# A hybrid decoder trunk: attention's 256-column products as three fp32r products, with the residual kept in DRAM meanwhile

## The chip, the cores and the metric

The kernel runs on one core of a Trainium2 chip. The metric is the device time of one execution in microseconds (us), as the median of several runs. Engines are called by the profile's names: PE is TensorE (matrix products; PEld its loads of the stationary operand), DVE is VectorE, ACT is ScalarE, POOL is GpSimd, SP is SyncE, whose queue issues nearly all DMAs here. SBUF is the on-chip memory of 128 partitions, PSUM the memory that products are written to.

## The reference

Two layers on 256 tokens of width 2048, in float32. Layer 0 mixes tokens with a gated MLP, layer 1 with a "forgetting" attention; a convolutional FFN of width 5632 follows each, and a last norm ends it. The change touches the attention of layer 1 only: 16 heads of 128 columns, two blocks of 128 queries, causal.

```
for i in range(S // Q_BLOCK):          # two query blocks
    lo, hi = i * Q_BLOCK, (i + 1) * Q_BLOCK
    s = einsum(q[lo:hi], k[:hi]) * scale + c[lo:hi, None] - c[None, :hi]
    p = softmax(where(causal, s, -inf))
    outs.append(einsum(p, v[:hi]))
o = concat(outs) * sigmoid(g);  h = h + o @ w_out
```

So a head has three 128 x 128 blocks of scores: queries 0-127 against keys 0-127, and queries 128-255 against both halves of the keys.

## The kernel before

**The stream.** All large weights pass through one stream of chunks of 128 x 1024 floats (512 KB). `Stream.run` goes through them: it issues the load of the chunk six ahead (SP), splits the chunk three ahead into a rounded part `whi` (ACT, L112) and a remainder `wlo` (DVE, L113), both of the type fp32r, then issues the products of the current chunk (PE, L213), and then calls `advance`, which takes every unfinished side task (a Python generator) one step, in the order in which they were started. The instructions of a step stand on each engine's queue behind the split that was issued just before it. A weight product in full accuracy is three fp32r products (rounded by rounded, rounded by remainder, remainder by rounded); after 24 such products of 256 columns a chunk is done. There are four buffers for parts, so the split of the chunk three ahead begins once the PE is through with the chunk before the current one.

**The attention's side task.** `heads` is started just before the chunks of the value projection (kvf_v: 32 chunks in four blocks of 512 columns) and goes on into the gate projection (b_g). It works in rounds, one every four chunks: rounds 0 to 7 issue the score products of two heads and start a `softmax` task for each; from some round on a round also issues the value products of up to two heads whose weights have come back transposed. In a round the order on PE is: value products (L1164 to L1166: three products of 128 columns a head), then for each head the score products (L1170: first query block against 128 keys, L1171: second against 256). All are plain fp32 products. The output goes from PSUM to `q`'s place by ACT (L1174).

**Softmax.** The even head's task reads the scores from PSUM one advance after the round (DVE L1122, then row maxima L1124), takes exponentials one advance later (ACT L1127), and normalises (L1129, L1131), transposes in blocks of 32 (L949) and sends the rows through DRAM (SP, L956 and L960) after that. The odd head's task does the same two advances later, so its score reading falls into the last advance before the next round. The two score buffers in PSUM (`mp`) are reused every round: a round's odd scores need the reading of the odd scores of the round before. Evictions of the value projection's blocks (ACT L1052) fall right behind the rounds 1, 3, 5 and 7, since a block has eight chunks. The key normalisation of the last key block (L1016 to L1025, L949) runs while the first chunks of kvf_v are streamed.

**The residual.** `h` ([128, 16, 256] float32, 2 MB) stays in SBUF from the input to the output. It is read by `kv_operand` before the attention and next read and written by `residual` in the output projection (b_out) after the gate projection.

Of the kernel before, what the change touches and what calls it, by code (L numbers as in the profile page):

```python
# [10 lines left out]
F32 = mybir.dt.float32  # L11
F32R = mybir.dt.float32r
# [5 lines left out]
P = 128  # L18
# [116 lines left out]
class Phase:  # L135


    def __init__(self, tc):
        self.tc, self.ctx, self.pool, self.name = tc, None, None, None

    def open(self, name):
        if self.name == name:
            return
        self.close()
        self.ctx = ExitStack()
        self.pool = self.ctx.enter_context(self.tc.tile_pool(name=name, bufs=1))
        self.name, self.kept = name, {}
# [30 lines left out]
def build(ctx, tc, d, out):  # L178
# [10 lines left out]
    h = const.tile([P, KD, T], F32, name="h")  # L189
# [201 lines left out]
    def residual(p, gain, scale=token_scale):  # L391

        def done(ps, both):
            hh = h[:, 2 * p:2 * p + 2, :]
# [577 lines left out]
    def kv_operand():  # L972
        assert state["prepared"]
        att("X2")
        nc.vector.tensor_tensor(att("gain"), column(C_QNORM), column(C_KNORM), op=OP.mult)
        for _ in range(3):
            yield
        for kt in range(KD):
            prep(att("X2"), kt, C_KVNORM)
            for _ in range(1 + kt % 2):  # L980
                yield

# [123 lines left out]
    def heads():  # L1106

        q, k, v, ccol = att("q"), att("k"), att("v"), att("ccol")
        rows, waiting = {}, []
# [26 lines left out]

        for hd in range(2):
            fetch(hd)
        for _ in range(3):
            yield  # L1140
        n = 0
        while state["done"] < NH:
# [11 lines left out]
            go = [hd for hd, _ in waiting if hd < state["v"]][:2]  # L1154
            if not pair and len(go) < min(2, NH - state["done"]):
                yield
                continue
            if go or pair:
                between()
            o = main_ps()[:, 0, :] if go else None  # L1160
            for i, hd in enumerate(go):
                pT = waiting.pop(0)[1]
                oo, vv = o[:, i * T:(i + 1) * T], v[:, :, hd * P:(hd + 1) * P]
                nc.tensor.matmul(oo[:, :P], vv[:, 0, :], pT[:, :, 0, :], start=True, stop=True)  # L1164
                nc.tensor.matmul(oo[:, P:], vv[:, 0, :], pT[:, :, 1, :], start=True, stop=False)  # L1165
                nc.tensor.matmul(oo[:, P:], vv[:, 1, :], pT[:, :, 2, :], start=False, stop=True)  # L1166
            for hd, L in pair.items():
                S = misc_ps()[:, :3 * P]
                kk = k[:, hd // 4, :, hd % 4, :]
                nc.tensor.matmul(S[:, :P], q[:, hd, :P], kk[:, :4], start=True, stop=True)  # L1170
                nc.tensor.matmul(S[:, P:], q[:, hd, P:], kk, start=True, stop=True)  # L1171
                s.start(softmax(hd, S, L))
            for i, hd in enumerate(go):
                nc.scalar.activation(q[:, hd, :], o[:, i * T:(i + 1) * T], AF.Copy)  # L1174
                state["done"] += 1
            for _ in range(4):
                yield
            n += 2

# [16 lines left out]
    state = {"normed": False, "layer": 0, "v": 0, "done": 0, "gates": 0, "mixed": 0, "scaled": 0, "summed": 0, "added": 0,  # L1196
             "prepared": False, "wide": [8, 2]}
    cd = dram.tile([NH, T], F32, name="cd")

# [52 lines left out]
    ph.close()  # L1252

# [67 lines left out]
```

## Time and profile before

| | |
|---|---|
| median of 3 runs | 2165.07 us (2164.87 to 2165.72) |
| profiled execution | 2165.71 us |
| its span on the core | 2164.0 us |
| instructions | 45230 |
| mean granted TensorE clock | 0.999 |
| read and written in HBM | 432.29 and 15.22 MB |
| score products L1170, L1171 | first at 1173.55 us, last round at 1267 us |
| value products L1164 | 1198.1 to 1303.9 us |

A page of the profile names groups by source line, engine, operation and tiles (out<-in). Products overlap at their ends, so the pitch from start to start is what one costs. An idle time and its releaser stand in brackets behind the row that followed it. A product in fp32 shows as two records, one in fp32r as one.

### The profile page before, as it was taken

The page shows a single profiled execution, that of the slowest core. Times are in us where ns is not written, and L with a number is a line of the kernel's source. Part 1 is how long each engine was busy: PE and PEld are TensorE (multiplying, and loading weights), DVE is VectorE, ACT ScalarE, POOL GpSimd, SP SyncE. Part 2 cuts the span into 40 slices and gives each one's busy share as a digit, 9 for nine tenths or more (in the row PEclk, how much of TensorE's full clock was granted, in tenths as well). Part 3 has the DMA queues.
Part 4 walks back from the last instruction along what each step waited for, and adds up shares of the span by engine and source line. Part 5 has one row for each costly group of instructions (what it writes and reads, how often), then busy time and mean ns, then how long its engine had stood idle before and what let it go on. Part 6 is the DMA issues. An engine that isn't in the chain of part 4 may idle for free.

```text
span 2164.0 us, 45230 instructions
## 1 busy us (share of the span) xinstructions
PE 2154.6 (100%) x18572; PEld 2137.7 (99%) x18572; DVE 1632.0 (75%) x2362; ACT 1199.0 (55%) x1644; POOL 27.5 (1%) x46
## 2 busy tenths in 40 slices
PE   9999999999999999999999999999999999999998
PEld 9999999999999999999999999999999999999998
DVE  6696687777777699977777676668777777779997
ACT  6664455555555555554545665545555555555555
POOL 0000000000000000000001200000000000000000
PEclk9999999999999999999999999999999999999999
DMA  8686566666666567677778876666766666666665
GB/s 313 188 248 199 194 198 194 192 196 188 202 195 192 175 199 227 224 230 185 243 233 268 238 218 200 189 217 200 266 195 194 192 195 192 196 192 186 205 205 166
DMA packets 157551, 450.47 MB, mean 208 GB/s; under 512 B 26064, under 2 KB 48352, under 8 KB 156960
## 3 DMA queue, kind: packets, MB, share of 16 engines
q1 hardware_dynamic: 155808, 443.63, 65.8%
q0 software_dynamic: 1072, 3.41, 0.6%
q8 instruction: 145, 2.38, 0.5%
q10 hardware_dynamic: 464, 0.55, 0.1%
q14 instruction: 62, 0.51, 0.1%
HBM read 432.29 MB, written 15.22 MB: 207 GB/s over the span
## 4 chain that ended last, share of the span: by engine, by line
PE 99%; DVE 0%; ACT 0%; issue 0%; POOL 0%; DVEq 0%; ACTq 0%; POOLq 0%
PE ps L213 97%; PE mp L213 1%; PE mp L1171 0%; PE mp L776 0%; PE ps L1165 0%; PE ps L1166 0%; PE ps L1164 0%; PE mp L1170 0%; ACT sq L437 0%; DVE h L743 0%; DVE h L436 0%; DVE h L737 0%; PE mp L408 0%; ACT fin_t L729 0%; DVE fin_t L733 0%
## 5 line engine op out<-in xcount | busy, mean ns | idle before, releaser
L113 DVE TENSOR_TENSOR wlo<-raw,whi 128x1024 fp32r<-128x1024 f32 (+1 forms) x732 | 887.8, 1219 | 287.1 <-ACT whi L112 283.9
L112 ACT ACTIVATE whi<-raw 128x1024 fp32r<-128x1024 f32 (+1 forms) x732 | 770.2, 1058 | 589.5 <-PE ps L213 471.4
L213 PE MATMUL ps<-X,whi 128*128 128x256 f32 (+1 forms) x6466 | 823.7, 280 | 0.0
L213 PEld LDWEIGHTS ps<-X,whi 128*128 128x128 f32 x6466 | 775.4, 188 | 6.8
L213 PE MATMUL ps<-X,wlo 128*128 128x256 f32 x3328 | 445.1, 276 | 0.0
L213 PEld LDWEIGHTS ps<-X,wlo 128*128 128x128 f32 x3328 | 409.8, 188 | 1.7
L213 PE MATMUL ps<-whi,ffn_H 128*128 128x256 f32 (+1 forms) x1852 | 303.2, 277 | 0.0
L213 PEld LDWEIGHTS ps<-whi,ffn_H 128*128 128x128 f32 x1852 | 255.5, 188 | 0.7
L213 PE MATMUL ps<-whi,X 128*128 128x256 f32 (+1 forms) x1336 | 221.5, 279 | 0.0
L213 PE MATMUL ps<-wlo,ffn_H 128*128 128x256 f32 (+1 forms) x924 | 192.1, 277 | 0.0
L213 PEld LDWEIGHTS ps<-whi,X 128*128 128x128 f32 x1336 | 187.3, 188 | 1.4
L920 DVE SCALAR_TENSOR_TENSOR ffn_room<-ffn_room,col 128x255 f32<-128x255 f32 x352 | 161.9, 481 | 6.4
L213 PE MATMUL ps<-whi,att_X 128*128 128x256 f32 (+2 forms) x970 | 164.3, 285 | 0.0
L213 PEld LDWEIGHTS ps<-wlo,ffn_H 128*128 128x128 f32 x924 | 144.2, 188 | 0.2
L213 PE MATMUL ps<-wlo,X 128*128 128x256 f32 (+1 forms) x666 | 144.3, 279 | 0.0
L389 DVE TENSOR_TENSOR ffn_room<-ps,rB 128x512 f32<-128x512 f32 x76 | 52.5, 691 | 114.4 <-PE ps L213 114.4
L213 PEld LDWEIGHTS ps<-whi,att_X 128*128 128x128 f32 x970 | 135.3, 188 | 3.5
L916 ACT ACTIVATE ffn_room<-ffn_room,col 128x256 f32<-128x256 f32 x176 | 96.3, 595 | 53.2 <-DVE ffn_room L389 53.2
L213 PEld LDWEIGHTS ps<-wlo,X 128*128 128x128 f32 x666 | 106.3, 188 | 0.4
L213 PE MATMUL ps<-wlo,att_X 128*128 128x256 f32 (+2 forms) x476 | 105.4, 286 | 0.0
L90 ACT ACTIVATE whi<-raw 128x768 fp32r<-128x768 f32 x46 | 39.0, 848 | 68.0 <-PE ps L213 54.7
L213 PEld LDWEIGHTS ps<-wlo,att_X 128*128 128x128 f32 x476 | 75.4, 188 | 1.0
(223 smaller groups left out, 1669.1 us busy)
## 6 DMA issues: line engine op xcount, KB each, us to landing
raw<-up SPq DMA_DIRECT2D x352, 512.0 KB, 4.2
raw<-down SPq DMA_DIRECT2D x154, 512.0 KB, 4.2
raw<-a_in_u SPq DMA_DIRECT2D x32, 512.0 KB, 4.4
raw<-a_out SPq DMA_DIRECT2D x32, 512.0 KB, 3.9
raw<-b_q SPq DMA_DIRECT2D x32, 512.0 KB, 4.7
raw<-kvf_v SPq DMA_DIRECT2D x32, 512.0 KB, 4.9
raw<-b_g SPq DMA_DIRECT2D x32, 512.0 KB, 4.2
raw<-b_out SPq DMA_DIRECT2D x32, 512.0 KB, 3.9
```

Source lines behind the costliest of these rows:

```text
L90: self.nc.scalar.activation(hi[:, cols], src[:, cols], AF.Copy)
L112: self.nc.scalar.activation(h, raw, AF.Copy)
L113: self.nc.vector.tensor_tensor(l, raw, h.bitcast(F32), op=OP.subtract)
L213: nc.tensor.matmul(o, a, b, start=start, stop=stop, skip_group_check=True)
L389: nc.vector.tensor_tensor(a, src, rB[:, None, :].to_broadcast([P, 2, T]), op=OP.mult)
L916: nc.scalar.activation(c[:, m, :], a[:, m, :], AF.Identity, scale=w[2], bias=column(C_CONVB + l * 2 * KF + f))
L920: nc.vector.scalar_tensor_tensor(c[:, m, n:], a[:, m, :T - n], w[k], c[:, m, n:], op0=OP.mult, op1=OP.add)
```

## The change

1. In a round, the products of 256 columns are made as three fp32r products. On the score side that is the second query block against all 256 keys. On the value side the first value block meets both query blocks' weights, so that two products of 128 columns become one of 256 (three in fp32r). The second value block (128 columns) and the first query block's scores (128 columns) stay in fp32.
2. The rounded parts are written by ACT, the remainders by DVE: for queries and keys in `query_parts`, for values and weights in `weight_parts`. Both are called in the four steps between two rounds, where there were four bare `yield`s. One set of buffers each, shared by the two heads of a round.
3. On PE all fp32r products of a round come first, value side before score side, and then the fp32 ones.
4. The heads of a round's value products are fixed earlier, when their parts are made, so the first value products come in round 3 and not in round 2.
5. The parts need room in SBUF. `h` moves into a pool of its own on the other side of SBUF, is stored in DRAM in eight DMAs by `kv_operand` (after its last reading, two advances apart), gives its place to the parts, and is loaded back in eight DMAs when `heads` is through.

```diff
+    side = Phase(tc, "right")
+    side.open("h0")
+    h = side.keep("h", [P, KD, T])
...
+        for i in range(8):
+            yield
+            yield
+            nc.sync.dma_start(kept[:, 2 * i:2 * i + 2, :], h[:, 2 * i:2 * i + 2, :])
+        state["kept"] = True
+
+    def taken_back():
+        nonlocal h
+        side.open("h1")
+        h = side.keep("h", [P, KD, T])
+        for i in range(8):
+            yield
+            nc.sync.dma_start(h[:, 2 * i:2 * i + 2, :], kept[:, 2 * i:2 * i + 2, :])
+        state["kept"] = False
...
+        def query_parts(n):
+
+            qq, kk = q[:, n:n + 2, P:], k[:, n // 4, :, n % 4:n % 4 + 2, :].rearrange("p t h j -> p h t j")
+            kv = [kp[:, i].rearrange("p h (t j) -> p h t j", t=8) for i in range(2)]
+            nc.scalar.activation(qp[:, 0], qq, AF.Copy)
+            nc.scalar.activation(kv[0], kk, AF.Copy)
+            yield
+            nc.vector.tensor_tensor(qp[:, 1], qq, qp[:, 0].bitcast(F32), op=OP.subtract)
+            nc.vector.tensor_tensor(kv[1], kk, kv[0].bitcast(F32), op=OP.subtract)
+
+        def weight_parts():
+
+            take = [hd for hd, _ in waiting if hd < state["v"]][:2]
...
+                nc.scalar.activation(vp[:, 0, i], v[:, 0, hd * P:(hd + 1) * P], AF.Copy)
+                nc.scalar.activation(pp[:, 0, i].rearrange("p (b r j) -> p r b j", b=2, r=4), pT[:, :, :2, :], AF.Copy)
+            yield
...
+                nc.vector.tensor_tensor(vp[:, 1, i], v[:, 0, hd * P:(hd + 1) * P], vp[:, 0, i].bitcast(F32),
+                                        op=OP.subtract)
+                hi, lo = (pp[:, l, i].rearrange("p (b r j) -> p r b j", b=2, r=4) for l in range(2))
+                nc.vector.tensor_tensor(lo, pT[:, :, :2, :], hi.bitcast(F32), op=OP.subtract)
+
+        def three(o, stat, mov, start, stop):
+            for j, (x, y) in enumerate(((0, 0), (0, 1), (1, 0))):
+                mm(o, stat[:, x], mov[:, y], start and j == 0, stop and j == 2)
...
-        for _ in range(3):
-            yield
+        yield
+        yield from query_parts(0)
+        yield
...
-            for i, hd in enumerate(go):
-                pT = waiting.pop(0)[1]
-                oo, vv = o[:, i * T:(i + 1) * T], v[:, :, hd * P:(hd + 1) * P]
-                nc.tensor.matmul(oo[:, :P], vv[:, 0, :], pT[:, :, 0, :], start=True, stop=True)
-                nc.tensor.matmul(oo[:, P:], vv[:, 0, :], pT[:, :, 1, :], start=True, stop=False)
-                nc.tensor.matmul(oo[:, P:], vv[:, 1, :], pT[:, :, 2, :], start=False, stop=True)
+            S = {hd: misc_ps()[:, :3 * P] for hd in pair}
+            for i, (hd, pT) in enumerate(go):
+                three(o[:, i * T:(i + 1) * T], vp[:, :, hd % 2], pp[:, :, hd % 2], i == 0, False)
+            for hd in pair:
+                three(S[hd][:, P:], qp[:, :, hd % 2], kp[:, :, hd % 2], True, False)
+            for i, (hd, pT) in enumerate(go):
+                nc.tensor.matmul(o[:, i * T + P:(i + 1) * T], v[:, 1, hd * P:(hd + 1) * P], pT[:, :, 2, :],
+                                 start=False, stop=True, skip_group_check=True)
             for hd, L in pair.items():
...
-            for _ in range(4):
-                yield
+            yield
+            if n + 2 < NH:
+                yield from query_parts(n + 2)
+            else:
+                yield
+            yield from weight_parts()
+            yield
             n += 2
+        s.start(taken_back())
```

The order on PE in round 4, before (att_v and att_rows are the value products' operands, att_q and att_k those of the scores; what a row waits for stands behind it):

```order
L1164 MATMUL ps<-att_rows,att_v 128x128 [waits DMAHW7_49,PE_49]
L1165 MATMUL ps<-att_rows,att_v 128x128
L1166 MATMUL ps<-att_rows,att_v 128x128
L1164 MATMUL ps<-att_rows,att_v 128x128 [waits DMAHW6_49]
L1165 MATMUL ps<-att_rows,att_v 128x128
L1166 MATMUL ps<-att_rows,att_v 128x128
L1170 MATMUL mp<-att_k,att_q 128x128 [waits DMAHW4_49,DVE_49]
L1171 MATMUL mp<-att_k,att_q 128x256
L1170 MATMUL mp<-att_k,att_q 128x128 [waits DVE_49,PE_49]
L1171 MATMUL mp<-att_k,att_q 128x256
```

The same round with the change (parts_pv and parts_qk are the new buffers of parts):

```order
L216 MATMUL ps<-parts_pv_14606,parts_pv_14605 128x256 [waits PE_49,Activation_49]
L216 MATMUL ps<-parts_pv_14606,parts_pv_14605 128x256 [waits DVE_49]
L216 MATMUL ps<-parts_pv_14606,parts_pv_14605 128x256
L216 MATMUL ps<-parts_pv_14606,parts_pv_14605 128x256 [waits Activation_49]
L216 MATMUL ps<-parts_pv_14606,parts_pv_14605 128x256 [waits DVE_49]
L216 MATMUL ps<-parts_pv_14606,parts_pv_14605 128x256
L216 MATMUL mp<-parts_qk_14604,parts_qk_14603 128x256 [waits PE_49]
L216 MATMUL mp<-parts_qk_14604,parts_qk_14603 128x256 x2
L216 MATMUL mp<-parts_qk_14604,parts_qk_14603 128x256 [waits DVE_49,PE_49]
L216 MATMUL mp<-parts_qk_14604,parts_qk_14603 128x256 x2
L1226 MATMUL ps<-att_rows,att_v 128x128 [waits DMAHW0_49]
L1226 MATMUL ps<-att_rows,att_v 128x128 [waits DMAHW7_49]
```

Two fp32 score products (L1229) follow. The odd head's scores, with their wait for DVE, now stand behind nine products, and the last value products (L1226) have only the two fp32 score products behind them.

DVE in the last advance before a round that has value products, with the change (L1185 and L1188 are the new subtractions; L1154 to L953 normalise and transpose the even head's weights; L1147 is the odd head's score reading, L1122 before):

```order
L113 TENSOR_TENSOR wlo<-raw,whi 128x1024 [waits DMAHW4_49,Activation_49]
L1185 TENSOR_TENSOR parts_pv_14605<-att_v,parts_pv_14605 128x128
L1188 TENSOR_TENSOR parts_pv_14606<-att_rows,parts_pv_14606 128x4x2x32 [waits DMAHW6_49]
L1185 TENSOR_TENSOR parts_pv_14605<-att_v,parts_pv_14605 128x128
L1188 TENSOR_TENSOR parts_pv_14606<-att_rows,parts_pv_14606 128x4x2x32 [waits DMAHW5_49]
L1154 RECIPROCAL att_sm<-att_sm 128x2
L1156 TENSOR_SCALAR att_big<-att_big,att_sm 128x128 [waits DVE_49]
L1156 TENSOR_SCALAR att_big<-att_big,att_sm 128x256
L953 STREAM_TRANSPOSE att_turned<-att_big 128x3x4x32 [waits DMAHW6_49,DMAHW1_49,DMAHW7_49,DMAHW0_49,DVE_49]
L1147 SCALAR_TENSOR_TENSOR att_big<-mp,att_big 128x384 [waits Pool_49]
```

The four subtractions stand between the split and the softmax work that was next to it before; two more (queries and keys) stand behind the split one chunk earlier.

DVE ahead of round 0, with the change (L1048 and L953 are the key normalisation of the last key block, L1025 and L949 before):

```order
L113 TENSOR_TENSOR wlo<-raw,whi 128x1024 [waits DMAHW0_49,Activation_49]
L1048 TENSOR_TENSOR att_big<-ps,att_hr 128x512 [waits DVE_49]
L953 STREAM_TRANSPOSE att_turned<-att_big 128x4x4x32 [waits DMAHW4_49,DMAHW2_49,DVE_49]
L113 TENSOR_TENSOR wlo<-raw,whi 128x1024 [waits DMAHW1_49,Activation_49]
L1048 TENSOR_TENSOR att_big<-ps,att_hr 128x512
L953 STREAM_TRANSPOSE att_turned<-att_big 128x4x4x32 [waits DMAHW2_49,DVE_49]
L1169 TENSOR_TENSOR parts_qk_14603<-att_q,parts_qk_14603 128x256
L1170 TENSOR_TENSOR parts_qk_14604<-att_k,parts_qk_14604 128x512
```

The first subtractions for queries and keys, which round 0 reads, stand behind both transposes of that normalisation; before, round 0 read nothing from DVE's queue.

More of the change, by code (lines that the diff above doesn't have):

```diff
@@ L135, with __init__ @@
 class Phase:
-    def __init__(self, tc):
+    def __init__(self, tc, side=None):
         self.tc, self.ctx, self.pool, self.name = tc, None, None, None
+        self.side = {"side": side} if side else {}
     def open(self, name):
@@ L145, in open @@
         self.ctx = ExitStack()
-        self.pool = self.ctx.enter_context(self.tc.tile_pool(name=name, bufs=1))
+        self.pool = self.ctx.enter_context(self.tc.tile_pool(name=name, bufs=1, **self.side))
         self.name, self.kept = name, {}
@@ L393, in done @@
         def done(ps, both):
+            assert not state["kept"]
             hh = h[:, 2 * p:2 * p + 2, :]
@@ L981, in kv_operand, with part_places @@
                 yield
+        for i in range(8):
[11 more added lines that the diff above has]
+        state["kept"] = False
+    def part_places(which):
+        side.open("parts")
+        return [side.keep(f"{which}{n}", [P, 2, 2, n], F32R) for n in (P, T)]
     def with_forget(src, x, done):
@@ L1106, in heads @@
     def heads():
+        assert state["kept"]
         q, k, v, ccol = att("q"), att("k"), att("v"), att("ccol")
-        rows, waiting = {}, []
+        rows, waiting, ready = {}, [], []
+        (qp, kp), (vp, pp) = part_places("qk"), part_places("pv")
         def fetch(hd):
@@ L1135, in softmax @@
                                 lambda dst: waiting.append((hd, dst.rearrange("p r (b j) -> p r b j", b=3))))
+        def query_parts(n):
[8 more added lines that the diff above has]
+            take = [hd for hd, _ in waiting if hd < state["v"]][:2]
+            for hd in take:
+                pT = waiting.pop(0)[1]
+                i = hd % 2
+                assert all(i != x % 2 for x, _ in ready)
+                ready.append((hd, pT))
+                nc.scalar.activation(vp[:, 0, i], v[:, 0, hd * P:(hd + 1) * P], AF.Copy)
+                nc.scalar.activation(pp[:, 0, i].rearrange("p (b r j) -> p r b j", b=2, r=4), pT[:, :, :2, :], AF.Copy)
+            yield
+            for hd, pT in ready[len(ready) - len(take):]:
+                i = hd % 2
+                nc.vector.tensor_tensor(vp[:, 1, i], v[:, 0, hd * P:(hd + 1) * P], vp[:, 0, i].bitcast(F32),
[5 more added lines that the diff above has]
+                mm(o, stat[:, x], mov[:, y], start and j == 0, stop and j == 2)
         for hd in range(2):
             fetch(hd)
-        for _ in range(3):
-            yield
+        yield
+        yield from query_parts(0)
+        yield
         n = 0
@@ L1153, in heads @@
                     fetch(hd + 2)
-            go = [hd for hd, _ in waiting if hd < state["v"]][:2]
-            if not pair and len(go) < min(2, NH - state["done"]):
+            if not pair and len(ready) < min(2, NH - state["done"]):
+                yield from weight_parts()
                 yield
                 continue
+            go, ready[:] = ready[:], []
             if go or pair:
@@ L1193, in g_done @@
         return done
-    state = {"normed": False, "layer": 0, "v": 0, "done": 0, "gates": 0, "mixed": 0, "scaled": 0, "summed": 0, "added": 0,
+    state = {"normed": False, "layer": 0, "v": 0, "done": 0, "gates": 0, "mixed": 0, "scaled": 0, "summed": 0, "added": 0, "kept": False,
              "prepared": False, "wide": [8, 2]}
     cd = dram.tile([NH, T], F32, name="cd")
+    kept = dram.tile([P, KD, T], F32, name="kept")
     nc.scalar.dma_start(col[:, :C_KVNORM], d["col"][:, :C_KVNORM])
@@ L1252, in build @@
     ph.close()
+    side.close()
 def feat_chunks(w, order=None):
```

12 lines of the change are left out of this document (5 added, 7 removed).

## The prediction

> **What bounds the kernel now.** I read the page's busy times first, then the chain of waits, then TensorE's own list of waits.
>
> ```profile
> PE 2154.6 (100%) x18572; PEld 2137.7 (99%) x18572; DVE 1632.0 (75%) x2362; ACT 1199.0 (55%) x1644; POOL 27.5 (1%) x46
> ...
> PE 99%; DVE 0%; ACT 0%; issue 0%; POOL 0%; DVEq 0%; ACTq 0%; POOLq 0%
> ```
>
> ```profile
> PE mp L776 <- POOL ident L1207: 1.5, 1, 1.5
> ```
>
> The chain is TensorE for 99% of the span, and the last row is the whole list of what TensorE ever waited for: 1.5 us at the start. So what the rounds lose or gain in TensorE time reaches the end one for one, and each new wait of TensorE costs its full length. VectorE and ScalarE matter only where TensorE would have to wait for them. The question is therefore double: how much TensorE time the new products save, and whether their operands are ready.
>
> **What the products cost.** The time line of TensorE around round 4 (start, length of the merged group, count):
>
> ```profile
> 1222.16 0.39 PE L213 MATMUL ps<-wlo,att_X 128*128 128x256 f32 x2
> ...
> 1224.20 0.39 PE L213 MATMUL ps<-wlo,att_X 128*128 128x256 f32 x2
> ...
> 1224.65 0.38 PE L1164 MATMUL ps<-att_rows,att_v 128*128 128x128 f32 x2
> ...
> 1225.77 0.39 PE L1166 MATMUL ps<-att_rows,att_v 128*128 128x128 f32 x2
> 1225.99 0.39 PE L1170 MATMUL mp<-att_k,att_q 128*128 128x128 f32 x2
> 1226.22 0.60 PE L1171 MATMUL mp<-att_k,att_q 128*128 128x256 f32 x2
> 1226.65 0.38 PE L1170 MATMUL mp<-att_k,att_q 128*128 128x128 f32 x2
> 1226.87 0.60 PE L1171 MATMUL mp<-att_k,att_q 128*128 128x256 f32 x2
> ```
>
> Lengths overlap, so I count from start to start. From 1222.16 to 1224.20 lie 18 fp32r products of 256 columns (three times two remainders and four rounded parts): 2.04 / 18 = 0.113 us each. From 1224.65 to 1225.99 lie six fp32 products of 128 columns, each shown as two records: 0.223 each. The fp32 product of 256 columns takes 1226.65 - 1226.22 = 0.43.
>
> Per head the value side gives up two of 0.223 for three of 0.113: 0.446 - 0.340 = 0.107 saved. The score side gives up one of 0.43: 0.43 - 0.34 = 0.09. Sixteen heads: 16 x 0.197 = **3.15 us saved**. A full round shrinks from 8 x 0.223 + 2 x 0.43 = 2.65 to 12 x 0.113 + 4 x 0.223 = 2.25. The new products have the shape and type of the weight products, so I take their price; the bounds are 0.11 (one of the two records of an fp32 product of 128) and 0.223 (both), which would make the saving 3.5 or turn it into a loss of 7.4.
>
> **The parts, and who waits for them.** Each round needs new work ahead of it: on ScalarE four to six copies, on VectorE a subtraction of 256 and one of 512 columns (query and key, two advances ahead), then two of 128 and two of 256 (values and weights, one advance ahead). VectorE between rounds 4 and 5, with idle time before a row in brackets:
>
> ```profile
> 1228.69 1.22 DVE L113 TENSOR_TENSOR wlo<-raw,whi 128x1024 fp32r<-128x1024 f32 x1 [2.25 <-ACT whi L112]
> 1229.84 0.15 DVE L1129 RECIPROCAL att_sm<-att_sm 128x2 f32<-128x2 f32 x1
> 1230.03 0.55 DVE L1131 TENSOR_SCALAR att_big<-att_big,att_sm 128x128 f32<-128x128 f32 x2
> 1230.62 0.58 DVE L949 STREAM_TRANSPOSE att_turned<-att_big 128x384 f32<-128x384 f32 x1
> 1231.12 0.52 DVE L1122 SCALAR_TENSOR_TENSOR att_big<-mp,att_big 128x384 f32<-128x384 f32 x1
> 1231.67 0.61 DVE L1124 TENSOR_REDUCE att_mx<-att_big 128x1 f32<-128x128 f32 x2
> 1232.20 1.22 DVE L113 TENSOR_TENSOR wlo<-raw,whi 128x1024 fp32r<-128x1024 f32 x1
> 1234.12 1.23 DVE L113 TENSOR_TENSOR wlo<-raw,whi 128x1024 fp32r<-128x1024 f32 x1 [0.70 <-ACT whi L112]
> 1235.26 0.16 DVE L1129 RECIPROCAL att_sm<-att_sm 128x2 f32<-128x2 f32 x1
> 1236.54 0.52 DVE L1122 SCALAR_TENSOR_TENSOR att_big<-mp,att_big 128x384 f32<-128x384 f32 x1
> ```
>
> Start to start, 1024 columns take 1.15 us and a 128 with a 256 take 0.59, which makes some 0.09 us plus 1.04 ns a column: 0.36 for 256, 0.62 for 512, 0.22 for 128. So the query and key subtractions take 0.98, those of values and weights 1.16, together 2.14 a round. Two of the operands (keys, weights) come in runs of 32 columns; the transpose of 384, which writes such runs, takes 0.50 where this rule gives 0.49. Half speed for them is the upper bound, rival C.
>
> The row that decides is the last one. It is the odd head's softmax reading its scores out of PSUM, done at 1236.54 + 0.52 = 1237.06, and it frees the buffer that the odd head's score product of round 5 needs. That product (the second L1170) came at 1240.26, so it had 3.2 us to spare:
>
> ```profile
> 1238.27 0.38 PE L1164 MATMUL ps<-att_rows,att_v 128*128 128x128 f32 x2
> ...
> 1240.26 0.38 PE L1170 MATMUL mp<-att_k,att_q 128*128 128x128 f32 x2
> ```
>
> Now the same round with the change, counted from the end of round 4 (1226.87 + 0.43 = 1227.30). ScalarE's rows carry the start:
>
> ```profile
> 1226.19 0.66 ACT L1174 ACTIVATE att_q<-ps 128x256 f32<-128x256 f32 x2 [1.61 <-PE ps L1166]
> ...
> 1227.61 1.05 ACT L112 ACTIVATE whi<-raw 128x1024 fp32r<-128x1024 f32 x1
> ...
> 1232.05 0.40 ACT L1127 ACTIVATE att_big<-att_big,att_mx 128x128 f32<-128x128 f32 x1 [0.65 <-DVE att_mx L1124]
> ...
> 1233.02 1.06 ACT L112 ACTIVATE whi<-raw 128x1024 fp32r<-128x1024 f32 x1
> ```
>
> The output copies L1174 wait for the last value product. It ended 1.31 us before the end of the round (2 x 0.223 + 2 x 0.43); now only two fp32 score products follow it, 0.45. So the copies, and the split (L112, L113) queued behind them, come 0.86 later against the round's end: L113 at 1.39 + 0.86 = 2.25. Then softmax 1.28 and 1.08, the next split 1.14, the query and key subtractions 0.98: 2.25 + 1.15 + 1.28 + 1.08 + 1.14 + 0.98 = 7.88. ScalarE is ready with the next L112 at the same time (exponentials from 5.81, 0.97, split 1.06: 7.84), so the 0.70 of idle time is used up. Split 1.15, values and weights 1.16, reciprocal to transpose 1.28, scores read 0.52: done at 11.99. TensorE reaches round 5 at 1238.27 - 1227.30 = 10.97, and the odd scores are now behind nine products of 0.113 instead of 1.99 us of work: 11.99, with the weight load 0.11 ahead at 11.88. The 3.2 us of cover are gone: **0.1 us of wait**.
>
> In rounds 4 and 6 one thing more stands ahead, the eviction of a value block after rounds 3 and 5:
>
> ```profile
> 1241.23 1.26 ACT L1052 ACTIVATE att_v<-ps,rcol 128x512 f32<-128x512 f32 x2
> 1242.37 1.07 ACT L112 ACTIVATE whi<-raw 128x1024 fp32r<-128x1024 f32 x1
> ```
>
> It holds the split back 1242.37 - 1241.23 = 1.14, and VectorE has no idle time left to make it good: done at 13.13, **1.25 us of wait** in each of the two. Round 2 has the eviction ahead too, but no value parts:
>
> ```profile
> 1186.48 0.38 PE L1170 MATMUL mp<-att_k,att_q 128*128 128x128 f32 x2
> ```
>
> ```profile
> 1188.75 1.23 DVE L113 TENSOR_TENSOR wlo<-raw,whi 128x1024 fp32r<-128x1024 f32 x1 [2.15 <-ACT whi L112]
> ```
>
> Round 1 ended at 1186.48 + 0.22 + 0.43 = 1187.13 and will be 0.18 shorter, so that split begins 1.80 after its end; the same chain without value parts is done at 10.38, and the odd scores need it at 10.97 + 0.34 - 0.11 = 11.20: no wait. Before round 3 no output copies are due (round 2 has no value products any more), which takes 0.86 off 11.99: no wait either. After round 7 no scores are left, and the value parts alone are done before TensorE needs them.
>
> Round 0 is a place of its own. The key normalisation of the last block is then still on VectorE, and the first subtractions come behind it:
>
> ```profile
> 1173.55 0.38 PE L1170 MATMUL mp<-att_k,att_q 128*128 128x128 f32 x2
> ```
>
> ```profile
> 1172.18 1.18 DVE L113 TENSOR_TENSOR wlo<-raw,whi 128x1024 fp32r<-128x1024 f32 x1
> 1173.29 0.68 DVE L1025 TENSOR_TENSOR att_big<-ps,att_hr 128x512 f32<-128x512 f32 x1
> 1174.00 0.71 DVE L949 STREAM_TRANSPOSE att_turned<-att_big 128x512 f32<-128x512 f32 x1
> 1174.64 2.32 DVE L113 TENSOR_TENSOR wlo<-raw,whi 128x1024 fp32r<-128x1024 f32 x2
> ```
>
> Before, round 0 needed nothing of VectorE. Now its second product reads the keys' remainders, and these are done at 1174.64 + 0.98 = 1175.62, while TensorE is there at 1173.6: **2.0 us of wait**. The bounds are 0 (none of the queue ahead of it) and 2.5 (strided at half speed).
>
> Queued behind each of these waits on TensorE is only its own stream; the splits run three chunks ahead.
>
> [...]
>
> **The moves of the residual.** Eight stores and eight loads of 256 KB each join SyncE's queue, one between weight loads. For the stores:
>
> ```profile
> 1060.00:1120.00 60.00, 60.00 (x511) 59.51 (x510) 43.21 (x74) 30.14 (x39) 0.00 (x0) 1.00 0.74 232
> ACT whi L112 <- DMA raw<-kvf_k: 7.2, 4, 3.1
> ```
>
> Over this stretch (third from the right: the granted clock, then DMA share and GB/s) the engines have 26% left: 232 / 0.74 x 0.26 = 81 GB/s, 4.9 MB in 60 us, for 2.1 MB. ScalarE waited for a key weight load up to 3.1 us, but its split runs three chunks ahead (3 x 2.73 less 1.06 and 1.23 is 5.9 us). I take 0; without that lead the stores' 2.1 MB at 232 / 0.74 GB/s would cost 6.7. The loads back fall after round 10, into the gate product, with 20 chunks before the first reader; 0 too. The rooms' first writers wait for stores issued 50 us earlier, the first load back for products four chunks old: 0.
>
> **Sum.** -3.15 + 2.0 + 2 x 1.25 + 2 x 0.1 = **+1.55 us**. The profiled execution took 2165.71 us (span 2164.0), so 2167.3 on its own time; the three runs shown have 2165.07, so **2166.6**. Whatever lies within 0.2%, 4.3 us, is what a measurement of this kernel cannot tell from no change; I forecast no change.
>
> **The rivals.**
> A, the forecast: waits in rounds 0, 4 and 6, 3.5 to 6 us together: 2165.4 to 2167.9. Chance 0.56.
> B, the gain stands: ScalarE and VectorE come early enough and at most 1.2 us is lost: 2161.9 to 2163.1. For it: rounds 5 and 7 miss by only 0.1 in my count, so a VectorE 1 us faster would clear all but round 0. Against it: every duration comes from the same loop, and round 0's queue is plain. Chance 0.22.
> C, slower: subtractions whose operand is cut into runs of 32 (keys, weights) go at half speed, 0.53 more in each set. Round 0 loses 0.53 more, rounds 4 to 7 1.06 each, round 3 0.4: +5.2, 2171.8. It decides from about 0.3 us a set, where rounds 5 and 7 wait too. Against it: the transposes write in such runs at 1.3 ns a column. Chance 0.08.
> D, the stores delay weight loads past the splits' lead; at 6.7 less the 2.8 that is left of 5.9 after a wait of 3.1, 3.9 us on top of A: 2170.5. Chance 0.04.
> E, the change doesn't do what it says: fp32r products beside fp32 ones take 0.223. The loss of 7.4 delays TensorE past the other waits but for round 0: 2165.07 + 7.4 + 2.0 = 2174.5. Against it: 0.113 holds wherever this shape runs. Chance 0.02.
> F, TensorE's granted clock falls after round 0's wait. The row above grants 1.00, and no wait here is long enough to show a fall. A chunk of 2.73 us at half clock would cost 2.7 more: 2169.3. Chance 0.03. [...]
> The remaining 0.05 is for what I have not seen.
>
> Faster by over 0.2% (under 2160.7) would need more than the whole saving: 0.02. Slower by over 0.2% (over 2169.4) are C, D, E and a tail: 0.12. Within: 0.86. The range takes in B and A and stops short of C: 2161.9 to 2169.5; A's own range stands above.
>
> **What would show it.** TensorE's list of waits, now one row, should show parts_qk products waiting for VectorE: 2.0 us once near 1173.6, and some 1.2 us near 1223 and 1250. Rounds without a wait should last 2.25. VectorE's subtractions should read 0.36 and 0.62 start to start, and the odd head's score reading should end about 12 us after a round, 13.1 after an eviction. The forecast is wrong if round 0 starts on time, if the two late rounds wait under 0.5 us, or if TensorE waits for a weight split at 1060 to 1130.

## The result and the profile after

The change is slower. Its median is 2170.24 us (2168.35 to 2173.78, 12 runs) beside 2165.91 for the kernel before (2164.87 to 2168.04, 12 runs): a ratio of 1.0022, with an interval of 1.0013 to 1.0031. That is 4.3 us more. The forecast was 2166.6 in a range up to 2169.5. The profiled execution took 2172.16 us, 2170.4 of them its span; it is one of the three longest of the twelve.

TensorE is still busy for 99% of the span. This is the first row of the page (busy time of each engine, share of the span, instructions):

```profile
PE 2156.1 (99%) x18572; PEld 2138.7 (99%) x18572; DVE 1648.4 (76%) x2410; ACT 1212.9 (56%) x1692; POOL 25.4 (1%) x46
```

VectorE and ScalarE have 16 and 14 us more work; it matters only where TensorE waits for it. The new waits show in TensorE's list of waits (who waited for whom: total, times, longest):

```profile
PE mp L216 <- DVE parts_qk L1170: 2.5, 1, 2.5
PE mp L216 <- DVE att_big L1147: 2.2, 2, 1.1
...
PE ps L216 <- DVE wlo L113: 0.2, 1, 0.2
```

The list of before had only the 1.5 us at the start. The first row is round 0's wait for the keys' remainders, the second the two late readings of the odd head's scores, in rounds 4 and 6. Both were in the prediction.

To see what the attention gains or loses as a whole I take two places that exist in every kernel here: the first product of round 0, and the first weight product behind the last value round. Before, round 0 starts at 1173.55 (a row in the prediction). The other end of before, from TensorE's time line, and ahead of it the second weight product behind round 4, which is used further down:

```profile
1227.54 0.39 PE L213 MATMUL ps<-wlo,att_X 128*128 128x512 f32 x1
...
1304.35 2.11 PE L213 MATMUL ps<-X,whi 128*128 128x512 f32 x8
```

And with the change, round 0, rounds 3 and 4, the score products of round 5, and the same end:

```profile
1174.76 0.28 PE L216 MATMUL mp<-parts_qk,parts_qk 128*128 128x256 f32 x1
1177.59 1.43 PE L216 MATMUL mp<-parts_qk,parts_qk 128*128 128x256 f32 x5 [2.54 <-DVE parts_qk L1170]
1178.82 1.05 PE L1229 MATMUL mp<-att_k,att_q 128*128 128x128 f32 x4
...
1215.46 0.88 PE L216 MATMUL ps<-parts_pv,parts_pv 128*128 128x256 f32 x6
1216.18 0.88 PE L216 MATMUL mp<-parts_qk,parts_qk 128*128 128x256 f32 x6
1216.90 0.60 PE L1226 MATMUL ps<-att_rows,att_v 128*128 128x128 f32 x4
1217.34 0.61 PE L1229 MATMUL mp<-att_k,att_q 128*128 128x128 f32 x4
1217.71 0.48 PE L216 MATMUL ps<-whi,att_X 128*128 128x512 f32 x1
1218.03 0.40 PE L216 MATMUL ps<-wlo,att_X 128*128 128x512 f32 x1
...
1229.51 0.52 PE L216 MATMUL mp<-parts_qk,parts_qk 128*128 128x256 f32 x3
1231.15 0.60 PE L216 MATMUL mp<-parts_qk,parts_qk 128*128 128x256 f32 x3 [1.12 <-DVE att_big L1147]
...
1244.18 1.03 PE L216 MATMUL mp<-parts_qk,parts_qk 128*128 128x256 f32 x6
1245.05 0.60 PE L1226 MATMUL ps<-att_rows,att_v 128*128 128x128 f32 x4
...
1310.35 2.11 PE L216 MATMUL ps<-X,whi 128*128 128x512 f32 x8
```

The stretch lasts 1304.35 - 1173.55 = 130.80 before and 1310.35 - 1174.76 = 135.59 with the change: **4.79 us more**, where the prediction's sum has 1.55.

The list of waits shows less than the gaps. A product's record (0.28) runs past the pitch from product to product (0.12), so the idle time behind it reads 0.16 short: round 0's gap is 1177.59 - 1174.76 - 0.12 = 2.71, where the list has 2.54. A wait as short as that does not show in the list at all. In round 5 the six score products take 1245.05 - 1244.18 = 0.87 instead of the 0.72 of round 3.

A third loss is no wait. Five products after round 0's wait take from 1177.59 to 1178.82, 1.23 us; in round 3 six take 0.72. The windows of one microsecond (busy time of PE, PEld, DVE, ACT and POOL, granted TensorE clock, DMA share, GB/s) show why:

```profile
1176.00:1177.00 1.00, 0.00 (x0) 0.00 (x0) 1.00 (x3) 0.02 (x1) 0.98 (x3) 1.00 0.74 198
1177.00:1178.00 1.00, 0.41 (x2) 0.42 (x3) 1.00 (x2) 0.00 (x0) 0.00 (x0) 0.66 1.06 91
1178.00:1179.00 1.00, 1.00 (x6) 1.00 (x6) 1.00 (x2) 0.11 (x1) 0.00 (x0) 0.50 0.53 74
...
1180.00:1181.00 1.00, 1.00 (x4) 0.77 (x4) 0.88 (x3) 0.00 (x0) 0.00 (x0) 0.63 1.01 372
```

The granted clock falls to half at 1177.32 (a mean of 0.66 is 0.32 at full and 0.68 at half clock) and comes back at 1180.74: 3.4 us at half clock. TensorE worked in 3.15 of them, from 1177.59, so it lost some 1.6 us. This is rival F, which had a chance of 0.03.

VectorE, around round 0 and in front of round 4, for comparison with the prediction's chains:

```profile
1175.19 0.68 DVE L1048 TENSOR_TENSOR att_big<-ps,att_hr 128x512 f32<-128x512 f32 x1
1175.91 0.71 DVE L953 STREAM_TRANSPOSE att_turned<-att_big 128x512 f32<-128x512 f32 x1
1176.55 0.38 DVE L1169 TENSOR_TENSOR parts_qk<-att_q,parts_qk 128x256 fp32r<-128x256 f32 x1
1176.85 0.68 DVE L1170 TENSOR_TENSOR parts_qk<-att_k,parts_qk 128x512 fp32r<-128x512 f32 x1
...
1226.78 1.22 DVE L113 TENSOR_TENSOR wlo<-raw,whi 128x1024 fp32r<-128x1024 f32 x1
1227.92 0.28 DVE L1185 TENSOR_TENSOR parts_pv<-att_v,parts_pv 128x128 fp32r<-128x128 f32 x1
1228.12 0.42 DVE L1188 TENSOR_TENSOR parts_pv<-att_rows,parts_pv 128x256 fp32r<-128x256 f32 x1
...
1230.48 0.52 DVE L1147 SCALAR_TENSOR_TENSOR att_big<-mp,att_big 128x384 f32<-128x384 f32 x1
```

From start to start the subtractions take 0.30 here and 0.34 in the next rounds (queries), 0.60 (keys, 1226.18 to 1226.78), 0.20 (values) and, from 1228.12 to the next at 1228.46, 0.34 (weights). The odd reading before round 4 is done at 1230.48 + 0.52 = 1231.00. Round 3's last two fp32 products start at 1217.34, and 2 x 0.223 later the round ends at 1217.79, so it is done 13.2 after the round.

### The profile page after: what moved, and what is told of

The parts are those of the page before. It is cut to its first block, busy times and chain, and to the rows that moved or that the text cites. A ratio compares the mean times of both kernels' runs of the same rounds, so it can differ in the third digit from the quotient of the medians.

```text
span 2170.4 us, 45367 instructions
## 1 busy us (share of the span) xinstructions
PE 2156.1 (99%) x18572; PEld 2138.7 (99%) x18572; DVE 1648.4 (76%) x2410; ACT 1212.9 (56%) x1692; POOL 25.4 (1%) x46
## 4 chain that ended last, share of the span: by engine, by line
PE 91%; DVE 4%; DMA 3%; issue 1%; ACT 1%; SPq 1%; DVEq 0%; POOL 0%; ACTq 0%; POOLq 0%
PE ps L216 89%; DVE wlo L113 2%; PE mp L216 1%; DMA way_h<-ffn_turned 1%; DMA raw<-kvf_v 1%; DMA raw<-kvf_k 1%; SPq L960 0%; ACT whi L112 0%; DVE att_big L1048 0%; DVE ffn_turned L953 0%; PE mp L780 0%; DMA way_k<-att_turned 0%; DMA raw<-b_g 0%; DMA raw<-kvf_fk 0%; PE mp L1229 0%
```

## The experiments

The theory after this reading: the change loses in three places, to be taken away one at a time. (1) Round 0 waits for a queue on VectorE, and (2) the idle time of TensorE there halves its clock afterwards. (3) In rounds 4 and 6 the eviction of a value block, ahead of splits, copies and value parts, makes the odd reading late. The rivals are those of the prediction: the stores (D), and a clock that falls for a reason other than idle time. Below, "stretch" is the time between the two places above less the 130.80 of before, in the profiled execution. The kernel before had 2165.69, 2165.55 and 2165.65 in the three sets of runs (27 to 33 runs each) and 2165.91 beside the change, so medians of different sets are comparable to some 0.4 us.

**Round 0's parts earlier.** The query and key parts of round 0 are made by a task of their own, started by the key normalisation of block 2, so they stand ahead of the last block's normalisation.

```diff
+    def first_parts():
+        places["qk"], places["pv"] = part_places("qk"), part_places("pv")
+        yield from query_parts(0)
...
-        yield from query_parts(0)
+        yield
...
-        tok_block(d["kvf_k"][8 * blk - 8:8 * blk], lambda: att("X2"), head_norm("k", blk))
+        tok_block(..., then_parts(head_norm("k", blk)) if blk == 2 else head_norm("k", blk))
```

> The query and key parts of round 0 are made one key block earlier (about 20 us), all else as in the change. Theory (the trace of the change: 2.54 us of wait in round 0, then 3.4 us at half clock): the wait goes, and with it the fall of the clock: -2.5 - 1.5 = -4.0 us against the change, so about 2166.2. Rival 1 (the clock falls for another reason): only -2.5, 2167.7, and a stretch of 0.5 clock stays near 1178 us. Rival 2 (the loss lies in the moves of the residual): within 0.5 us of the change. The waits of 1.1 us in rounds 4 and 6 stay in every case.

Measured: 2166.64 us, ratio 1.0005 (0.9996 to 1.0014). Round 0's wait is gone from TensorE's list, and the granted clock stays at 1.00:

```profile
PE mp L216 <- DVE att_big L1172: 2.3, 2, 1.2
```

The stretch is +0.57 instead of +4.79. Round 0's wait with what follows it is worth 4.2 us in the profiles, 3.6 in the medians, and the gap itself is only 2.7 of it.

**The eviction one advance later.** `v_evict` gets a bare step ahead of its copies, so that they no longer stand in front of the split behind a round.

```diff
     def v_evict(blk):
         def done(ps):
+            yield
             v = att("v")
```

> The eviction of a value block begins one advance later than in the change, so it no longer stands ahead of the weight split right behind rounds 1, 3, 5 and 7. Theory: rounds 4 and 6 wait as little as rounds 5 and 7 (0.3 instead of 1.4 us each, restart included): -2.3 us against the change, about 2167.9; round 0 keeps its 2.5 us. Rival (VectorE is short of time altogether, not late by the eviction): rounds 4 and 6 still wait about 1 us, and the time is that of the change.

Measured: 2167.83 us, ratio 1.0011 (1.0002 to 1.0019), stretch +2.05. The waits of rounds 4 and 6 are gone from the list; these rounds last 2.54 us up to the next weight product instead of 3.60. Round 0's is there, shorter in this execution, on TensorE's time line and in the windows:

```profile
1173.30 0.28 PE L216 MATMUL mp<-parts_qk,parts_qk 128*128 128x256 f32 x1
1175.42 0.86 PE L216 MATMUL mp<-parts_qk,parts_qk 128*128 128x256 f32 x5 [1.85 <-DVE parts_qk L1171]
```

```profile
1175.00:1176.00 1.00, 0.58 (x5) 0.58 (x5) 1.00 (x2) 0.00 (x0) 0.00 (x0) 1.00 0.73 52
1176.00:1177.00 1.00, 1.00 (x9) 0.91 (x8) 1.00 (x2) 0.75 (x2) 0.00 (x0) 0.78 0.61 86
1177.00:1178.00 1.00, 1.00 (x4) 0.81 (x3) 1.00 (x2) 0.18 (x1) 0.00 (x0) 0.50 0.89 321
```

TensorE works again from 1175.42 at full clock; the clock falls at 1176.56, 1.14 us later. So here the fall does not come with the idle time but after it. And 1.85 us of idle time are enough, if it is the idle time that halves the clock; the kernels with fillers below test that.

**Both.**

> Both edits. Theory: -4.0 - 2.3 = -6.3 us against the change: about 2163.9, which is 2 us less than the kernel before. TensorE's list of waits shows neither a parts_qk product in round 0 nor over 0.4 us at the odd scores. Rival (the moves of the residual, or products dearer than 0.113 us, cost what is missing): 2165 to 2167, no better than before.

Measured: 2164.64 us, ratio 0.9995 (0.9986 to 1.0004), stretch -1.01. What is left of waits in the list, in round 1:

```profile
PE mp L216 <- DVE att_big L1173: 0.4, 1, 0.4
```

The late eviction and the early parts together turn the loss into a small gain that the medians cannot tell from no change. The theory had 0.7 us less, 2163.9.

**The moves alone.** The kernel before, with the residual stored and loaded back as in the change, and no parts.

```diff
+        for i in range(8):
+            yield
+            yield
+            nc.sync.dma_start(kept[:, 2 * i:2 * i + 2, :], h[:, 2 * i:2 * i + 2, :])
...
+        s.start(taken_back())
```

> The kernel before with the residual stored and loaded back as in the change, and nothing else: products in fp32, no parts. Theory: the moves cost 0 to 0.6 us (in the trace of the change a weight split came 0.35 us late near 1133 us, behind the stores): 2165.9 to 2166.5. Rival D (the stores delay weight loads past the splits' lead): +2 to +4 us, 2168 to 2170, and TensorE waits for weight splits between 1060 and 1140 us.

Measured: 2165.66 us, ratio 1.0002 (0.9993 to 1.0011), stretch 0.00. The medians show no cost, and the 3.9 us of rival D fall. The stretch says nothing of the stores, which are issued from 1067 to 1103 us, ahead of it. Between 1120 and 1140 us TensorE's products fall back by 0.52 us against those of the kernel before, at weight remainders; in the other profiled executions with the moves it is 0 to 0.7 between 1120 and 1160. That lies within the theory's 0 to 0.6 or close to it; that the stores cause it is not shown. From the end of the stretch to the end of the span both kernels take 859.64 us, so the loads back show no cost.

**TensorE kept busy through the wait.** Right behind round 0's first product come ten, and in a second kernel five, fp32 products of the identity, whose result nothing reads.

```diff
+                if hd == 0:
+                    mm(S[0][:, P:], qp[:, 0, 0], kp[:, 0, 0], True, False)
+                    for _ in range(10):
+                        mm(S[1][:, P:2 * P], ident, ident, True, True)
+                    mm(S[0][:, P:], qp[:, 0, 0], kp[:, 1, 0], False, False)
+                    mm(S[0][:, P:], qp[:, 1, 0], kp[:, 0, 0], False, False)
+                    continue
                 three(S[hd][:, P:], qp[:, :, hd % 2], kp[:, :, hd % 2], True, False)
```

> TensorE gets ten fp32 products of 128 columns on the identity (a result that nothing reads) right behind round 0's first product, where it waits for the keys' remainders: 10 x 0.223 = 2.2 us of the 2.5 us of wait are filled with work. The end of the wait is VectorE's and does not move. Theory (the granted clock falls because TensorE is idle): the clock stays 1.00 behind round 0, TensorE's list of waits shows some 0.3 us there, and the time is the change's 2170.2 less 1.4 = 2168.8. Rival (the clock falls for another reason, such as the place or the fp32r products there): still 0.50 for some 3.4 us, 2170.2.

> As the one before with five products: 1.1 us of the 2.5 us are filled, 1.4 us of idle time is left. This lies between the 1.1 us of rounds 4 and 6, after which the clock stayed at 1.00, and the 1.8 us after which it fell in the kernel with the later eviction. If the length of the idle time decides with a bound under 1.4 us, the clock falls and the time is 2170.2; if the bound lies over 1.4 us, it stays at 1.00 and the time is 2168.8.

Measured: 2169.54 us, ratio 1.0018 (1.0009 to 1.0027), with ten; 2169.22, ratio 1.0018 (1.0009 to 1.0026), with five. Round 0 with ten:

```profile
1175.59 0.28 PE L216 MATMUL mp<-parts_qk,parts_qk 128*128 128x256 f32 x1
1175.70 2.40 PE L216 MATMUL mp<-ident 128*128 128x128 f32 x20
1177.86 0.84 PE L216 MATMUL mp<-parts_qk,parts_qk 128*128 128x256 f32 x5
```

and one window over the same place:

```profile
1174.00:1184.00 10.00, 10.00 (x80) 9.54 (x79) 7.90 (x12) 5.44 (x13) 2.22 (x4) 1.00 0.81 264
```

The round comes no sooner, but the clock stays at 1.00 and the five products take 0.68 (the next one started at 1178.54) instead of 1.23. With five fillers 0.74 us of idle time was left (not the 1.4 expected, for round 0's wait was shorter in that execution), and the clock stayed at 1.00 too. The stretches are +2.77 and +2.64, 1.4 to 2.2 us under those of the change's two profiles (+4.79, and +4.17 below). In the medians the difference to the change is only 0.7 and 1.0, under the 1.4 expected; the intervals do not exclude either. The rows are sharper: from round 0's start to round 1's it takes 14.39 and 14.24 us, which is 2.28 and 2.13 more than in the kernel without waits (12.11, with the odd head's products last, below), about the gap alone (2.15 and 2.02). In the change it is 4.27 more, for a gap of 2.71. The place and the round's own products are those of the change, and only the idle time is filled, so the profiles say that idle time is the cause. The medians do not contradict it and are not sharp enough to confirm its size by themselves.

**One side alone.** First only the value side is made of parts, then only the score side.

```diff
-                three(S[hd][:, P:], qp[:, :, hd % 2], kp[:, :, hd % 2], True, False)
+                mm(S[hd][:, P:], q[:, hd, P:], k[:, hd // 4, :, hd % 4, :], True, False)
```

> Only the value products are made of parts; the scores of 256 columns are fp32 again, and no query or key parts are made. Theory: round 0 needs nothing of VectorE's queue, so its wait and the fall of the clock are gone; VectorE has 0.98 us less in a round, so the odd scores are read at 13.13 - 0.98 = 12.15 in rounds 4 and 6, about when TensorE needs them. Left is the saving of the value side, 16 x (0.446 - 3 x 0.12) = 1.4 us: 2165.7 - 1.4 = 2164.3. If the value parts alone hold the scores up as before, 2.3 us more: 2166.6.

Measured: 2167.65 us, ratio 1.0010 (1.0001 to 1.0019). The theory's 2164.3 was wrong and the second figure, 2166.6, nearer. The stretch is +0.9; the rest of the 2.1 us in the median is not placed. Round 0 is clean, but rounds 4 and 6 still wait:

```profile
PE mp L216 <- DVE att_big L1147: 2.0, 2, 1.0
```

VectorE lost 0.98 us of work a round and won next to nothing. Its row and ScalarE's ahead of round 4:

```profile
1221.96 1.23 DVE L113 TENSOR_TENSOR wlo<-raw,whi 128x1024 fp32r<-128x1024 f32 x1 [0.61 <-ACT whi L112]
...
1225.81 0.52 DVE L1147 SCALAR_TENSOR_TENSOR att_big<-mp,att_big 128x384 f32<-128x384 f32 x1
```

```profile
1220.88 2.00 ACT L112 ACTIVATE whi<-raw 128x1024 fp32r<-128x1024 f32 x2
```

VectorE now has 0.61 us of idle time, waiting for the rounded part that ScalarE writes behind the exponentials, and one of the weight subtractions takes 0.2 longer, for which the trace gives no reason. The prediction had both engines ready within 0.04 us of each other (7.84 and 7.88); taking work from one of them leaves the other. My expectation for this run forgot that.

```diff
-                three(o[:, i * T:(i + 1) * T], vp[:, :, hd % 2], pp[:, :, hd % 2], i == 0, False)
+                oo, vv = o[:, i * T:(i + 1) * T], v[:, 0, hd * P:(hd + 1) * P]
+                mm(oo[:, :P], vv, pT[:, :, 0, :], i == 0, True)
+                mm(oo[:, P:], vv, pT[:, :, 1, :], False, False)
```

> Only the score products are made of parts; the value products are fp32 again and no value or weight parts are made. Theory: round 0 waits 2.5 us and the clock falls, 1.4 us more; VectorE has 1.16 us less in the advance ahead of a round, so rounds 4 and 6 do not wait. The saving is 16 x (0.43 - 0.36) = 1.1 us: 2165.7 + 2.5 + 1.4 - 1.1 = 2168.5. Rival (the score parts alone hold up rounds 4 and 6): 2.3 more, 2170.8.

Measured: 2170.30 us, ratio 1.0021 (1.0012 to 1.0030), 1.8 over the theory's figure and near the rival's, but not for the rival's reason. TensorE's list has one row for the rounds:

```profile
PE mp L216 <- DVE parts_qk L1170: 2.8, 1, 2.8
```

Rounds 4 and 6 do not wait, and in the kernel before this one they did, so these waits hang on the value and weight parts. The clock fell here too (a mean of 0.89 from 1165 to 1180). Its stretch is +3.70; the theory's terms, with 2.8 for the wait and 1.6 for the clock, come to 3.3. Of the 4.75 us in the median some 0.3 lie outside the span: in all eleven runs the time is 2.0 to 2.1 us longer than the span, in the other kernels 1.7 to 1.8. The rest I cannot place.

**The odd head's products last.** In the two kernels below the odd head's three fp32r products stand behind the value products and the even head's fp32 scores. First on top of both mends, then on the change alone, and with them the change once more.

```diff
-            for hd in pair:
+            for hd in list(pair)[:1]:
                 three(S[hd][:, P:], qp[:, :, hd % 2], kp[:, :, hd % 2], True, False)
...
             for hd, L in pair.items():
+                if hd % 2:
+                    three(S[hd][:, P:], qp[:, :, 1], kp[:, :, 1], True, False)
```

> Round 0's parts earlier, the eviction one advance later, and now the odd head's three fp32r products behind the value products and the even head's fp32 scores of the same round. In rounds 1 and 2 they move back by one fp32 product of 0.223, in rounds 3 to 7 by five, 1.1 us. What was left of waits (0.4 us in round 1) shrinks to 0.2. Sum: 2165.7 - 2.5 + 0.2 = 2163.4, the products' saving nearly whole. If moving from one type of product to the other and back costs TensorE something of its own, rounds last over 2.33 us and the time stays at e3's 2164.6 or above.

Measured: **2164.40 us, ratio 0.9990 (0.9981 to 0.9999)**: faster than both kernels, by 1.25 us against before, where 2163.4 was expected. TensorE's list has no row for the attention's rounds any more. Round 3 and the end of the stretch, which began at 1174.36:

```profile
1210.68 0.88 PE L216 MATMUL ps<-parts_pv,parts_pv 128*128 128x256 f32 x6
1211.40 0.52 PE L216 MATMUL mp<-parts_qk,parts_qk 128*128 128x256 f32 x3
1211.76 0.60 PE L1242 MATMUL ps<-att_rows,att_v 128*128 128x128 f32 x4
1212.20 0.39 PE L1247 MATMUL mp<-att_k,att_q 128*128 128x128 f32 x2
1212.34 0.60 PE L216 MATMUL mp<-parts_qk,parts_qk 128*128 128x256 f32 x3
1212.78 0.38 PE L1247 MATMUL mp<-att_k,att_q 128*128 128x128 f32 x2
1212.92 0.48 PE L216 MATMUL ps<-whi,att_X 128*128 128x512 f32 x1
...
1302.36 2.11 PE L216 MATMUL ps<-X,whi 128*128 128x512 f32 x8
```

Round 3 lasts 1212.92 - 1210.68 = 2.24 up to the next weight product, and so do rounds 4 to 7. Twelve products of 0.12 and four of 0.223 come to 2.33, so going from one type of product to the other and back costs nothing that shows. The stretch lasts 1302.36 - 1174.36 = 128.00, which is 2.80 less than before. With no wait and no fall of the clock in it (behind rounds 0 and 2 to 5 the weight products of 512 columns with a remainder take 0.23 to 0.24), this is what the products save: **2.8 us**. The median shows 1.25 of it, and its interval reaches to 4. In the profiles the whole span is 2.0 shorter: 0.8 us are lost again between 1090 and 1140 us, ahead of the attention, for the most part at a wait for ScalarE and at weight remainders.

> The change with only that reordering. Rounds 4 and 6: the odd products are needed five fp32 products later, 5 x 0.223 = 1.1 us, the length of the wait, but the last value products, and with them the output copies and the split of the next chunk, also come 0.36 earlier against the round's end: some 0.1 us of wait left in each. [...] So the change's 2170.2 less 2.1 = 2168.1.

Measured: 2168.69 us, ratio 1.0011 (1.0002 to 1.0020), 0.6 over the 2168.1 expected; the stretch is +1.83. Round 0's wait is 2.0, and the clock falls: the mean of the execution reads 0.998, and the weight product at 1179.43 takes 0.43 us up to the next one, where one of the same shape at 1204.38 takes 0.23. Rounds 4 and 6 have no row left in TensorE's list; on the time line the odd products start some 0.4 us late, where 0.1 was expected.

> The change once more, beside the two reorderings: 2170.2 by its twelve runs so far. In the profile round 0 waits 2 to 2.8 us. [...]

Measured: 2170.42 us, ratio 1.0019 (1.0011 to 1.0028). Round 0's wait was 1.84 us in this execution and ended at 1175.55, and the windows read:

```profile
1175.00:1176.00 1.00, 0.46 (x4) 0.46 (x4) 1.00 (x2) 0.00 (x0) 0.00 (x0) 1.00 0.84 78
1176.00:1177.00 1.00, 1.00 (x10) 0.96 (x9) 1.00 (x2) 0.64 (x2) 0.00 (x0) 0.97 0.43 62
1177.00:1178.00 1.00, 1.00 (x4) 0.81 (x3) 1.00 (x2) 0.30 (x1) 0.00 (x0) 0.50 0.86 291
...
1180.00:1181.00 1.00, 1.00 (x9) 1.00 (x8) 0.00 (x0) 0.00 (x0) 0.00 (x0) 0.82 0.99 385
```

Half clock from 1176.94 to 1180.36, 3.4 us again, and it begins 1.4 us after TensorE went back to work. The stretch is +4.17, 0.62 less than in the first profile, about what round 0's wait was shorter (0.70).

**The clock in all runs.** For every run the record has the mean granted clock to three digits, and one fall of 3.4 us takes 0.0008 from it (half of 3.4 in a span of some 2167). In the seven kernels that do not wait in round 0, or fill the wait, it reads 0.999 in all 77 runs. In the five that wait there it reads 0.998 or less in 38 of 56. A 0.999 does not exclude a fall: the profiled execution with the later eviction reads 0.999 and has one. So in how many runs the clock falls cannot be counted. But with the fillers none of 22 runs is under 0.999, and of the change itself 17 of 23 are. This confirms the cause where the medians alone could not.

## Why the prediction was wrong

**The step that failed is the one on round 0's wait and the clock.** The prediction's sum priced the wait by its length alone and put the clock at nothing. It gave the fall of the clock, rival F, a chance of 0.03, for "no wait here is long enough to show a fall". TensorE's only wait in the kernel before is the 1.5 us at the start, so what a wait of 2.0 us in mid-stream does to the clock was the author's estimate; no run had shown it. Five profiled executions wait there for 1.84 to 2.82 us, and in all five the clock falls. In four of them the windows show half clock for 3.4 us; in the fifth, with the odd products last on the change alone, the weight product at 1179.43 shows it (0.43 us instead of 0.23). The rival's price was an estimate too, 2.7 us for a whole chunk at half clock; the windows of the change give 1.6, the half of the 3.15 us that TensorE worked in at half clock. Early parts remove both, for 3.6 us in the medians; the wait is 2.0 to 2.7 of it, by the gaps in the change's two profiles.

In the change's two profiles the half clock lasts from 1177.32 to 1180.74 and from 1176.94 to 1180.36, 3.42 us each. The first begins 0.3 us before TensorE goes back to work, the second 1.4 us after it. A wait of 1.84 us was enough. Waits of 1.0 to 1.2 us were not: over rounds 4 and 6 the windows show 1.00 in the change and in the kernels with the early parts, with the fillers and with the value side alone. What decides between 1.2 and 1.8 us, and what sets the moment of the fall, no run here shows.

**The other terms, in order:**

- The products: predicted -3.15, measured -2.80 in the kernel without waits. From a round's first product to the second weight product behind it, a full round lasts 1227.54 - 1224.65 = 2.89 before and 1218.03 - 1215.46 = 2.57 with the change: 0.32 saved, where the prediction has 2.65 - 2.25 = 0.40. In the kernel without waits it is 0.34, by 13.61 and 13.27 from round to round. Six fp32r products of a round take 0.72, which is 0.12 each and not 0.113. The kind of saving was right and its size a tenth too large; rival E falls.
- Round 0: predicted 2.0. Five executions waited 1.84, 1.85, 2.02, 2.54 and 2.82 by the list, some 0.16 more by the gaps; the middle one is the forecast. The queue was the one named: transpose L953, then L1169 and L1170.
- Rounds 4 and 6: predicted 1.25 each, measured 1.12 and 1.1; the chain's end was predicted 13.13 after the round and came at 13.2. Moving the eviction away took them off the list, as the chain said, and left 0.3 us in each (2.54 up to the next weight product, 2.24 in the kernel without waits). The same eviction was also said to cost nothing in round 2, and no wait showed there.
- Rounds 5 and 7: predicted 0.1 each. The list has no row for them, but round 5's six score products take 0.15 longer than round 3's, and against the kernel without waits the two rounds lose 0.20 and 0.15. The forecast was near.
- The subtractions: predicted 0.36, 0.62 and 0.22 from start to start, measured 0.34, 0.60 and 0.20. The 256 columns of the weights, in runs of 32, take the same 0.34 as those of the queries, so rival C falls.
- The moves: predicted 0; alone they measure 1.0002 (0.9993 to 1.0011). The 0.2 us in the change's list, for a weight remainder, belongs to the 0 to 0.7 us that the profiles show ahead of the attention.

**The sum again.** The kernel with the odd head's products last and both mends has no wait in its rounds. Taking its times from one round's start to the next from those of the change's first profile shows where the 4.79 us lie:

| | predicted | measured |
|---|---|---|
| the products | -3.15 | -2.80 |
| round 0, the wait (its gap) | 2.0 | 2.71 |
| round 0, the clock | 0 | 1.56 |
| rounds 4 and 6 | 2.5 | 2.80 |
| rounds 5 and 7 | 0.2 | 0.35 |
| rounds 1 to 3 | 0 | 0.17 |
| sum | 1.55 | 4.79 |

Round 0 takes 16.38 us up to round 1 with the change and 12.11 in the other kernel; less the gap of 2.71, 1.56 is left for the clock, which agrees with the 1.6 of the windows. The 0.17 of rounds 1 to 3 may be short waits or the other order of the products; that is open.

In the medians the forecast missed by 3.6 us. Of these 0.84 are its starting point: the three runs of before that it went by have a median of 2165.07, the twelve beside the change 2165.91. With the clock's 1.6 alone added, the forecast would have been 2168.2, inside its own range. The other rows add 1.7 in the profiled execution, 0.7 of it in round 0's wait.

## What to carry to other kernels

A new wait of the engine that sets the time is not priced by its length alone: look at the granted clock over the wait and the five microseconds behind it, and where it is at half, add half of the time that TensorE works in it. With the waits of 1.84 to 2.82 us here it fell, to 0.50 for 3.4 us in four profiles, which cost 1.6 us in the change's first. With waits of 1.0 to 1.2 us it stayed at 1.00, and they cost about their gap (2.80 us for two of some 1.3 in the change). Where a step needs operands from another engine's queue, the cheap mend is to put the making of them ahead of that queue's long work, or other work of TensorE ahead of the wait; here both together, and one eviction moved by one step, turned a loss of 4.3 us into a gain of 1.25. Where two engines come ready within a few hundredths of a microsecond, taking work from one of them buys next to nothing. And a list of waits is not the sum of the gaps: the short ones show only in the times from round to round.

## What the runs showed of the hardware

With round 0's waits of 1.84 to 2.82 us the granted clock fell to half, and not always during the wait: it went to 0.50 some 1.1 us (the later eviction) and 1.4 us (the change once more) after TensorE had gone back to work, and 0.3 us before it went back in the change's first profile. In the first two the five products right behind the wait took 0.70 and 0.68 us, in the third 1.23. So the products that pay for a wait need not be the ones behind it on the time line, and the list of waits shows nothing of the cost.
